# Loading the first x as eight transfers of 16 partitions with step 8

## The chip, the core and the metric

One core of a Trainium2 chip. The metric is the device time of the program in microseconds (us); less is better. A profile also gives the span from the first to the last instruction, about 2 us less than that time (262 against 260.2 us in the profiled run before).

## The reference

```python
batch, m, k, n = 16, 512, 768, 1024
x: [16, 768, 512] float32      y: [16, 768, 1024] float32
np.einsum('bkm,bkn->bmn', x, y).astype(np.float32)
```

Sixteen products of 512 x 768 by 768 x 1024. The core reads 75.5 MB and writes 33.55 MB.

## The kernel before

Row k = 6p + ko of a batch lies in partition p, so each partition of an x is one contiguous run of 12288 bytes in memory, and of a y one of 24576 bytes. All transfers are issued by SyncE (SP), between device memory and the SBUF, the core's buffer of 128 partitions. VectorE (DVE) casts x and y to bf16, TensorE (PE) multiplies, ScalarE (ACT) copies the products out of PSUM, where TensorE leaves them.

```python
    x_v = x.rearrange("b (p ko) m -> b p ko m", ko=KT)      # KT = 6, P = 128
    ...
    def wide_dma(key, dst, src, dram_rows, load):
        if key not in made:                                 # the first of its kind: plain,
            made[key] = nc.sync.dma_start(dst, src)         # one read per partition
            return made[key]
        ...                                                 # later ones: a copy whose reads
                                                            # span dram_rows partitions
    for b in range(B):
        i = b % 2
        if b >= 2:
            nc.sync.wait_ge(cast, nx[b - 2])
        wide_dma("x", xs[i][:], x_v[b], 4, True).then_inc(sx[i], 16)
        if b >= 2:
            nc.sync.wait_ge(cast, nx[b - 2] + parts(b - 2))
        wide_dma("y", ys[i][:], y_v[b], 2, True).then_inc(sy[i], 16)
        if b >= LAG:
            store(b - LAG)
    ...
    for b in range(B):                                      # VectorE
        i = b % 2
        n = 16 * (b // 2 + 1)
        ...
        nc.vector.wait_ge(sx[i], n)
        nc.vector.tensor_copy(xb[:, i], xs[i][:]).then_inc(cast, 1)
        nc.vector.wait_ge(sy[i], n)
        ...
```

The whole kernel:

## Time and profile before

| | before |
|---|---|
| time, median of 3 runs | 262.55 us (262.53 to 262.94) |
| span of the profiled run | 260.2 us |
| share of 16 DMA engines' time filled | 98.3% |
| moved over the span | 419 GB/s |
| first x cast, first y cast begin at | 7.23 us, 14.91 us |

The prediction below shows the lines of this profile. They are to be read in this order: the shares of the engines (none of the compute engines is full), the DMA row (full in all slices but the first and the last), then the start of the stream. In the tables by window a line holds the stretch, its length, five pairs of busy time and number of instructions (PE, PEld, DVE, ACT, POOL), the granted TensorE clock, the DMA share and the GB/s. A packet is counted where it starts, so short windows scatter around the mean.

### The profile page before, as it was taken

The numbers are of one execution on the slowest core, as the hardware profiler recorded it, in microseconds if no ns is written. First come the engines' busy times: TensorE is split into PE (matmuls) and PEld (weight loads), VectorE is DVE, ScalarE is ACT, GpSimd is POOL, SyncE is SP. The second block draws the span as 40 slices with busy tenths as digits, with TensorE's granted clock in tenths as the row PEclk, the third lists the DMA queues.
The fourth block names the chain that finished last, engine by engine and source line by source line (L and its number), as shares of the span: only waits on it lengthen the run. The fifth ranks groups of instructions, "written<-read, shape, count | busy, mean of one in ns | idle before, by whom it ended". The sixth has DMA issues, their size and how long they took to land. (4 is left out here: it accounts for less than half of the span.)

```text
span 260.2 us, 2506 instructions
## 1 busy us (share of the span) xinstructions
PE 188.3 (72%) x768; PEld 90.3 (35%) x768; DVE 82.0 (32%) x33; ACT 61.1 (23%) x33; POOL 0.2 (0%) x4
## 2 busy tenths in 40 slices
PE   0019999998938959499491995949869697785930
PEld 0004555554513525244250352514424243442410
DVE  0261644525241152511425214252232523125000
ACT  1000442243220222203222022220412204031220
POOL 0000000000000000000000000000000000000000
PEclk9999999999995979979999597997968989997985
DMA  7999989999999999999999999999999999999995
GB/s 272 418 476 408 476 378 469 393 368 461 438 398 469 388 479 423 411 441 393 458 431 441 433 388 464 408 436 446 396 456 418 464 416 423 451 385 431 438 403 227
DMA packets 4514, 109.07 MB, mean 419 GB/s; under 512 B 768, under 2 KB 768, under 8 KB 768
## 3 DMA queue, kind: packets, MB, share of 16 engines
q1 hardware_dynamic: 4512, 109.05, 98.3%
q14 instruction: 2, 0.02, 0.0%
HBM read 75.50 MB, written 33.55 MB: 419 GB/s over the span
## 5 line engine op out<-in xcount | busy, mean ns | idle before, releaser
L149 PE MATMUL ps<-yb,xb 128*128 x768 | 188.3, 411 | 61.0 <-PEq L144 61.0
L149 PEld LDWEIGHTS ps<-yb,xb 128*128 x768 | 90.3, 118 | 158.5 <-issue 92.6
L165 ACT COPY ob<-ps 128x2048 f32<-128x2048 f32 x32 | 59.8, 1869 | 184.8 <-PE ps L149 184.8
L127 DVE CAST yb<-ys 128x6144 bf16<-128x6144 f32 (+1 forms) x17 | 53.8, 3171 | 86.5 <-DMA ys<-in_y_dram 86.5
L123 DVE CAST xb<-xs 128x3072 bf16<-128x3072 f32 x16 | 28.2, 1760 | 69.7 <-DMA xs<-in_x_dram 65.2
L165 ACT ACT_TABLE_LOAD x1 | 1.3, 1283 | 5.3 <-issue 5.3
L189 POOL MEMSET const-bfloat16-1.0<- 128x1 bf16 x1 | 0.1, 102 | 0.0
L189 POOL MEMSET const-uint8-127<- 128x1 uint8 x1 | 0.1, 102 | 0.0
L189 POOL MEMSET const-float32-1.0<- 128x1 f32 x1 | 0.1, 99 | 0.0
L189 POOL MEMSET const-float32-0.0<- 128x1 f32 x1 | 0.1, 98 | 0.2 <-issue 0.2
## 6 DMA issues: line engine op xcount, KB each, us to landing
ys<-in_y_dram SPq DMA_DIRECT2D x16, 3072.0 KB, 28.2
out_dram<-ob SPq DMA_DIRECT2D x16, 2048.0 KB, 32.6
xs<-in_x_dram SPq DMA_DIRECT2D x16, 1536.0 KB, 29.8
```

What stands on the lines that cost most here:

```text
L123: nc.vector.tensor_copy(xb[:, i], xs[i][:]).then_inc(cast, 1)
L127: nc.vector.tensor_copy(yb[:, i, ks], ys[i][:, ks]).then_inc(cast, 1)
L149: mm = nc.tensor.matmul(ps[g][:, m, nt], x_w[:, bass.ds(s, 1), kt, mo], yb[:, bass.ds(s, 1), kt, nt * NF:(nt + 1) * NF], start=(kt == 0), ...
L165: cp = nc.scalar.copy(ob[b % NO][:, g * HB:(g + 1) * HB].rearrange("p m (t f) -> p m t f", f=NF), ps[g][:])
L189: nc = _bacc.Bacc("TRN2", target_bir_lowering=False, num_devices=1)
```

## The change

Its intent: with a single transfer of 128 rows some of the DMA engines start up to 1 us later than others (by the packet records ten start at 1.98 to 2.08 us and six at 2.74 to 3.02). Eight transfers of 16 rows were meant to give each of the sixteen engines one row at a time, so that all begin at once. Each transfer adds 16 to the semaphore that VectorE waits for, so the seven further transfers add 112 to the number awaited. A side effect: the x of batch 1 is now the first of its kind, and so loaded plainly.

```diff
+    x_first = x_v[0].rearrange("(a c) k m -> a c k m", c=8)
+    for c in range(8):
+        nc.sync.dma_start(xs[0][c::8], x_first[:, c]).then_inc(sx[0], 16)
     for b in range(B):
         i = b % 2
         if b >= 2:
             nc.sync.wait_ge(cast, nx[b - 2])
-        wide_dma("x", xs[i][:], x_v[b], 4, True).then_inc(sx[i], 16)
+        if b > 0:
+            wide_dma("x", xs[i][:], x_v[b], 4, True).then_inc(sx[i], 16)
 ...
-        nc.vector.wait_ge(sx[i], n)
+        nc.vector.wait_ge(sx[i], n + (112 if i == 0 else 0))
```

## The prediction

Passages that no trace of this case bears out are cut, and the cuts are marked. Packets of a 16-row transfer with step 8 would take twice as long as the 0.46 us of the present load: that factor of two was my assumption, and the profile before did not show it; "sharing" is its name. That small transfers would let the late engines start on time was assumed too. The sum came to +2.7 us for the first x and +0.1 us for the small terms, +2.8 us and so 265.3 us, if packets are twice as long (case a), and to -0.4 us if they are not (case b).

> **What bounds the kernel now.** I read the page first (parts 2, 3, 5), then the chain of waits, then the queue's issues in order of time, then windows of one microsecond at the start and of ten at the end, and last the records of single DMA packets in the trace.
>
> Parts 1 to 3 of the page:
> ```profile
> PE 188.3 (72%) x768; PEld 90.3 (35%) x768; DVE 82.0 (32%) x33; ACT 61.1 (23%) x33; POOL 0.2 (0%) x4
> ...
> DMA  7999989999999999999999999999999999999995
> ...
> q1 hardware_dynamic: 4512, 109.05, 98.3%
> ...
> HBM read 75.50 MB, written 33.55 MB: 419 GB/s over the span
> ```
> No compute engine is full, but the row DMA has a 9 or an 8 in all slices except the first and the last, and the one queue that carries loads and stores fills 98.3% of the time of 16 DMA engines. Each engine moves 109.05 MB / 16 = 6.816 MB. The packet records give the unit costs: 12288 bytes take 460 ns (first x), 24576 bytes 912 ns (first y), 49152 bytes 1837 ns on average (all later loads), 16384 bytes 611 ns (stores). Per engine: 8 x 0.460 + 8 x 0.912 + 90 x 1.837 + 128 x 0.612 = 3.7 + 7.3 + 165.3 + 78.3 = 254.6 us. The first packets start at 1.98 us, so about 257 us is the earliest end. The DMA stream is the bound, and only the start, the end and the rate of the engines are left to win or lose.
>
> The view of the waits says the same from the other side, and the chain that ended last is only the tail:
> ```profile
> DVE yb L127 <- DMA ys<-in_y_dram: 86.5, 16, 5.9
> DVE xb L123 <- DMA xs<-in_x_dram: 65.2, 13, 7.2
> ```
> VectorE waits 152 us for loads. Nothing on the compute side is ever early enough to hold the DMA queue up: the page's part 6 shows loads issued 28 to 30 us before they land, so two to three transfers always stand in the queue.
>
> The start, from the timeline (start, duration, what):
> ```profile
> 0.95 0.39 SPq L72 DMA_DIRECT2D xs<-in_x_dram  x1
> 1.39 0.42 SPq L72 DMA_DIRECT2D ys<-in_y_dram  x1
> 1.86 0.54 SPq L72 DMA_DIRECT2D xs<-in_x_dram  x1
> 2.44 0.62 SPq L72 DMA_DIRECT2D ys<-in_y_dram  x1
> ...
> 7.23 1.76 DVE L123 CAST xb<-xs 128x3072 bf16<-128x3072 f32 x1 [7.23 <-DMA xs<-in_x_dram]
> ...
> 14.91 3.36 DVE L127 CAST yb<-ys 128x6144 bf16<-128x6144 f32 x1 [5.92 <-DMA ys<-in_y_dram]
> ```
> and the windows (last two columns: DMA share, GB/s):
> ```profile
> 1.00:2.00 1.00, 0.00 (x0) 0.00 (x0) 0.00 (x0) 0.00 (x0) 0.00 (x0) 1.00 0.19 37
> 2.00:3.00 1.00, 0.00 (x0) 0.00 (x0) 0.00 (x0) 0.00 (x0) 0.00 (x0) 1.00 0.81 160
> 3.00:4.00 1.00, 0.00 (x0) 0.00 (x0) 0.00 (x0) 0.00 (x0) 0.00 (x0) 1.00 0.83 344
> 4.00:5.00 1.00, 0.00 (x0) 0.00 (x0) 0.00 (x0) 0.00 (x0) 0.00 (x0) 1.00 1.12 479
> ```
> The reader should see that the stream reaches its full rate (some 430 GB/s) only after 3 us. The packet records say why: ten engines start between 1.98 and 2.08 us, but their first packets take 636 to 1516 ns instead of 460; six engines start only between 2.74 and 3.02 us. Eight engines end the first x at 6.09 to 6.46 us, eight at 6.75 to 6.85 us. A clean start would be 1.98 + 8 x 0.46 = 5.66 us. So 0.4 to 1.2 us per engine are lost there, and that is what the change is after.
>
> The end: by the packet records twelve engines end at 256.98 to 257.35 us and four at 257.92 to 258.56 us. The last store is issued at 251.2 us, and several of the faster engines stand idle for 0.3 to 1.1 us around then, because PE and the last copy release it; the slow four never idle, and they set the end.
>
> [...]
> [...] 12288 bytes in 460 ns are 26.7 GB/s per engine, all sixteen at once[...]
> [...] 0.39 us for the issue, first packet 1.03 us after its start, landing at about 7.2 us.
>
> **The change part by part.**
> 1. Removed: one issue of 128 rows (0.39 us). Added: eight of 16 rows, partitions c, c+8, ..., c+120. The cheapest issues of plain transfers here are 0.33 to 0.39 us, with 0.05 us between them, so a step of about 0.44 us. The first y is issued at 0.95 + 8 x 0.44 = 4.5 us instead of 1.39, and its first packets can start at 4.5 + 1.0 = 5.5 us. The engines come to it after 5.7 us at the earliest, so the issues are hidden; at 0.6 us each (like the fourth issue now) y could start only at 6.8 us, about where the late engines start it today.
> 2. [...] the six late engines should start at about 2.0 us: up to 0.8 us won for them[...].
> 3. [...] Then each packet takes about 2 x 0.46 = 0.92 us and the first x takes 8 x 0.92 = 7.4 us instead of 8 x 0.46 = 3.7. From 2.0 us, with some 0.3 us of the cold start left, all engines end it at about 9.7 us, against 6.3 and 6.8: 2.9 to 3.4 us later, call it 2.7 allowing for part of the sharing to go uneven.
> 4. Small terms: seven more semaphore packets per engine, 7 x about 6 ns = 0.04 us. The later loads are copies of the first plain one of their kind with widened reads; now x of batch 1 is that plain one, 8 x 0.460 = 3.68 us instead of 2 x 1.82 = 3.63: 0.05 us. Together 0.1 us.
>
> All this happens in the first 10 us on a stream that never idles later, so a shift of the engines passes to the end one for one; the last y, the last casts, PE and the last store follow the loads by the same amount. The sum is +2.7 + 0.1 = +2.8 us [...] and 0.1 - 0.5 = -0.4 us if not.
>
> **Rivals.**
> (a) [...] 262.55 + 2.8 = 265.3 us. [...]
> (b) No sharing, a clean start: the late engines gain 0.4 to 1.1 us, the early ones 0 to 0.7; the slowest gains about 0.5, less 0.1: 262.1 us. For: late starts are visible. [...]
> (c) The queue starves on the issues: steps of 0.6 us put y at 6.8 us or later, so 0 to 1 us lost: 263 us. For: the third and fourth issues took 0.54 and 0.62 us. Against: these had 128 rows behind 128 rows[...].
> (d) The gain is hidden by the end: if the chain over PE and the last store set the end, nothing would come through. It follows the last load, which shifts as well, so I give it little.
>
> **Range and chances.** I give (a) 60%, (b) and (d) 28%, (c) 12%. The prediction is the middle of the likelier case, 265.1 us; the range must reach from the clean start, 261.8, to full sharing with the whole cold start kept, 266.2. The 2% limits are 257.3 and 267.8 us; no case comes near either: within 2% 0.96, slower 0.03, faster 0.01.
>
> **What would show it right or wrong.** Right: eight issues of about 0.4 us from 0.95 us; sixteen engines starting near 2.0 us; packets of the first x at about 0.9 us and only some 215 GB/s between 3 and 9 us; the first x cast beginning at about 10 us and the first y cast at about 17.6 us instead of 14.91; all DMA after that as before. Wrong: packets of 460 ns in the first x and its cast before 7.2 us (then (b)), or gaps between the packets (then (c)). A change of the rate in the middle of the stream, where nothing was touched, would be outside of this reasoning.

## The result, and the profile after

| | before | after |
|---|---|---|
| time, median of 4 runs each | 262.54 us (262.36 to 262.94) | 266.34 us (265.98 to 266.74) |
| ratio | | 1.0143 (1.0123 to 1.0162) |
| span of the profiled run | 260.2 us | 264.6 us |
| first x cast, first y cast begin at | 7.23, 14.91 us | 11.02, 18.85 us |

A ratio is the mean time of one kernel's fast runs over that of the other's of the same rounds, so it isn't quite the ratio of the medians quoted. The loss is 3.8 us. The prediction said 265.1 us and a range up to 266.2; the time lies 0.14 us above the range, and the loss is half as large again as the 2.55 us forecast.

The page after, DMA parts:

```profile
DMA  6999998999999899899999999899998999999993
...
q1 hardware_dynamic: 4720, 109.06, 97.7%
...
HBM read 75.50 MB, written 33.55 MB: 412 GB/s over the span
```

The stream is as full as before nearly everywhere. "Busy" tells nothing of the loss: a slow packet counts as busy for as long as it takes. The bytes do tell.

The start, from the timeline after:

```profile
0.95 5.04 SPq L104 DMA_DIRECT2D xs<-in_x_dram  x8
...
6.03 0.58 SPq L72 DMA_DIRECT2D ys<-in_y_dram  x1
...
11.02 1.76 DVE L128 CAST xb<-xs 128x3072 bf16<-128x3072 f32 x1 [11.02 <-DMA xs<-in_x_dram]
...
18.85 3.36 DVE L132 CAST yb<-ys 128x6144 bf16<-128x6144 f32 x1 [6.07 <-DMA ys<-in_y_dram]
```

Eight issues take 5.04 us, 0.63 us from one to the next, where the prediction had 0.44. The first x is there 3.8 us later than before, the first y 3.9 us later: the whole loss is there before the first matmul.

The stretch from 4 to 9 us, before and then after:

```profile
4.00:9.00 5.00, 0.00 (x0) 0.00 (x0) 1.76 (x1) 1.28 (x1) 0.00 (x0) 1.00 1.04 447
```
```profile
4.00:9.00 5.00, 0.00 (x0) 0.00 (x0) 0.00 (x0) 1.28 (x1) 0.00 (x0) 1.00 1.04 218
```

The DMA share is 1.04 in both, the rate 447 against 218 GB/s. The packet records show the same one by one: of the 128 packets of the first x, the last 96 to start took 831 to 989 ns (before: 460 for nearly all). The 32 before them were shorter (458 to 871 ns).

The end, from the chain that ended last, before and then after:

```profile
237.05 12.25 PE ps L149 x48
...
249.33 1.87 ACT ob L165
```
```profile
241.37 10.74 PE ps L154 x48
...
252.13 1.87 ACT ob L170
```

The last matmuls begin 4.3 us later and the last copy 2.8 us later, because TensorE was granted a higher clock in the last batch after (1.00 against 0.86, 10.74 us for the same 48 matmuls instead of 12.25). That did not help: by the packet records the slowest DMA engine lands its last store at 263.33 us after and 258.93 us before, some 3 and 1.5 us behind the median engine, and the program waits for it (SyncE's last wait for stores: 4.1 us after, 2.5 before).

### The profile page after: what moved, and what is told of

Its sections match the earlier page's. It is cut to its first block, busy times and chain, and to the rows that moved or that the text cites. A ratio compares the mean times of both kernels' runs of the same rounds, so it can differ in the third digit from the quotient of the medians.

```text
span 264.6 us, 2513 instructions
## 1 busy us (share of the span) xinstructions
PE 187.7 (71%) x768; PEld 90.1 (34%) x768; DVE 82.0 (31%) x33; ACT 61.1 (23%) x33; POOL 0.2 (0%) x4
```

## The experiments

The theory: which partitions a transfer names sets the time of its packets. How much was my assumption before the runs: with 16 rows of step 8 twice the 0.46 us of the kernel before, with 16 contiguous rows four times, with step 7 mostly once. No trace shows a mechanism that would give these factors; the figures that stand without a rival's name are those of the theory. Rivals: the eight issues and small transfers themselves; the distance of the rows in memory; something of the start of the program only; and the side effect on the x of batch 1. Ten kernels were run, all of them as variants of the two above. Times are medians, "before" is that of the same call.

| run | first x is loaded as | time | before | ratio (95%) |
|---|---|---|---|---|
| a1_after_again | 8 x 16 rows, step 8 (the change) | 266.06 | 262.31 | 1.0144 (1.0127 to 1.0161) |
| a2_step1 | 8 x 16 rows, contiguous | 270.02 | 262.31 | 1.0283 (1.0266 to 1.0300) |
| a3_step7 | 7 x 16 rows, step 7, and 16 contiguous | 264.68 | 262.31 | 1.0087 (1.0070 to 1.0104) |
| a4_hbm_rows | as the change; memory rows contiguous (wrong result) | 265.94 | 262.31 | 1.0137 (1.0120 to 1.0153) |
| b1_late | as before; batch 8 as in the change | 266.70 | 262.67 | 1.0156 (1.0138 to 1.0174) |
| b2_step4 | 4 x 32 rows, step 4 | 263.10 | 262.67 | 1.0017 (0.9997 to 1.0037) |
| b3_free6 | 6 x 128 rows of 2048 bytes | 262.92 | 262.67 | 1.0017 (0.9994 to 1.0040) |
| b4_before_again | as before | 262.77 | 262.67 | 1.0000 (0.9982 to 1.0018) |
| c1_halves | 2 x 128 rows of 6144 bytes | 262.60 | 262.56 | 1.0005 (0.9992 to 1.0019) |
| c2_x1_plain | as before; x of batch 1 plain | 262.54 | 262.56 | 1.0001 (0.9987 to 1.0014) |

### The change again, for a second profile

No edit.

> The changed kernel itself, unaltered, for a second profile beside its variants. If the loss is fixed by the program: 266.0 to 266.7 us again, first-x packets near 0.9 us, the median engine 3.0 us later than before from batch 5 on. Open: whether one engine again lags the median by 3 us at the end. If that lag is chance of one execution, it differs in this profile while the median does not; if it belongs to the changed start, it is there again.

The time is 266.06 us. In the packet records the median engine lands the first y at 17.73 us (first profile after: 17.74; before: 14.39). The slowest engine again ends about 3 us behind the median (2.9; in the first profile 3.1). The loss is the program's, not one execution's.

Both profiles of the change also show that the packets that start fifth (65th to 80th by start) are shorter: their median is 0.86 and 0.85 us in the two profiles, against 0.95 and 0.94 us for the sixteen before them and 0.94 to 0.95 us for the last 32. Why was not shown.

### Contiguous rows

```diff
-    x_first = x_v[0].rearrange("(a c) k m -> a c k m", c=8)
     for c in range(8):
-        nc.sync.dma_start(xs[0][c::8], x_first[:, c]).then_inc(sx[0], 16)
+        rows = slice(16 * c, 16 * c + 16)
+        nc.sync.dma_start(xs[0][rows], x_v[0, rows]).then_inc(sx[0], 16)
```

> The same eight transfers of 16 rows, but partitions 16c to 16c+15 instead of every eighth. [...] first-x packets of about 1.84 us instead of 0.93, the first x ends at about 17 us instead of 9.8, the time is 266.3 + 7.4 = 273.7 us. Rival, cost of eight issues and small transfers: the issues are the same, so 266.3 us and packets of 0.93 us.

The same number of transfers of the same size, other partitions. In the timeline and the window from 4 to 12 us:

```profile
0.94 3.64 SPq L104 DMA_DIRECT2D xs<-in_x_dram  x8
...
15.66 1.76 DVE L128 CAST xb<-xs 128x3072 bf16<-128x3072 f32 x1 [15.66 <-DMA xs<-in_x_dram]
```
```profile
4.00:12.00 8.00, 0.00 (x0) 0.00 (x0) 0.00 (x0) 1.28 (x1) 0.00 (x0) 1.00 1.02 121
```

The issues are even cheaper than with step 8 (0.46 us from one to the next instead of 0.63), and the kernel is 4.0 us slower. From the third packet of each engine on, a packet took 1.60 to 1.64 us, and the rate fell to 121 GB/s. So the number of issues isn't the cause; which partitions a transfer names is. The size was a miss: I had expected 1.84 us and 273.7 us. The 1.84 us was four times 0.46, an assumption; why the packets took less was not shown.

### Step 7

```diff
-    x_first = x_v[0].rearrange("(a c) k m -> a c k m", c=8)
-    for c in range(8):
-        nc.sync.dma_start(xs[0][c::8], x_first[:, c]).then_inc(sx[0], 16)
+    for c in range(7):
+        nc.sync.dma_start(xs[0][c:112:7], x_v[0, c:112:7]).then_inc(sx[0], 16)
+    nc.sync.dma_start(xs[0][112:], x_v[0, 112:]).then_inc(sx[0], 16)
```

> Seven transfers of 16 rows with step 7 and a last one of the 16 contiguous rows left over. [...] most packets take 0.46 us and a few 0.92; the last transfer has [...] 1.84 us. The issues of 0.63 us then set the pace, the first x ends at about 8.5 us instead of 9.8, and the time is about 265.0 us. Rival, cost of eight issues: 266.3 us. Rival, the step in memory or in the buffer at all: packets of 0.93 us as with step 8.

Seven of the eight transfers now name every seventh partition, the last one 16 contiguous ones. From the timeline:

```profile
0.94 4.43 SPq L103 DMA_DIRECT2D xs<-in_x_dram  x7
5.42 0.58 SPq L104 DMA_DIRECT2D xs<-in_x_dram  x1
...
10.39 1.76 DVE L128 CAST xb<-xs 128x3072 bf16<-128x3072 f32 x1 [10.39 <-DMA xs<-in_x_dram]
```

The time is 264.68 us (expected: about 265.0), with as many issues and the same 0.63 us between them as in the change. The packets of the first seven transfers mostly took 0.46 to 0.84 us, a few up to 1.2: shorter than with step 8, but not the clean 0.46 for most of them that I had expected. The first x ended later than expected (its cast at 10.39 us); why was not shown. In no run did all packets of 16-row transfers take 0.46 us, so a part of what stands above 0.46 us here (the median of the first seven transfers is 0.63 us, as long as the step of the issues) may belong to 16-row transfers as such. It is too small to explain the 0.94 us of step 8.

### Contiguous rows in memory, step 8 in the SBUF

Its output is wrong, which doesn't matter for the time.

```diff
-    x_first = x_v[0].rearrange("(a c) k m -> a c k m", c=8)
     for c in range(8):
-        nc.sync.dma_start(xs[0][c::8], x_first[:, c]).then_inc(sx[0], 16)
+        nc.sync.dma_start(xs[0][c::8], x_v[0, 16 * c:16 * c + 16]).then_inc(sx[0], 16)
```

> Wrong result on purpose: partitions c, c+8, ... as in the changed kernel, but the rows read from memory are 16 contiguous ones. [...] nothing changes, packets 0.93 us, 266.3 us. Rival, the memory side (rows 98 KB apart read by 16 engines at once): packets fall towards 0.46 us and the time to about 264 us, where the pace of the issues holds it.

```profile
4.00:9.00 5.00, 0.00 (x0) 0.00 (x0) 0.00 (x0) 1.28 (x1) 0.00 (x0) 1.00 1.00 216
```

216 GB/s between 4 and 9 us and 265.94 us: nothing changed (the change: 218 GB/s, 266.06 us). The distance of the rows in memory is ruled out; what matters is which partitions are written: with the same rows read, contiguous partitions (a2_step1) gave 270.02 us. The issues stay at 0.59 us each too, against 0.42 us there, so the step of the partitions, not that of the rows in memory, made these issues dearer.

### The same in the middle of the stream

```diff
-        wide_dma("x", xs[i][:], x_v[b], 4, True).then_inc(sx[i], 16)
+        if b == 8:
+            x_eight = x_v[b].rearrange("(a c) k m -> a c k m", c=8)
+            for c in range(8):
+                nc.sync.dma_start(xs[i][c::8], x_eight[:, c]).then_inc(sx[i], 16)
+        else:
+            wide_dma("x", xs[i][:], x_v[b], 4, True).then_inc(sx[i], 16)
 ...
-        nc.vector.wait_ge(sx[i], n)
+        nc.vector.wait_ge(sx[i], n + (112 if i == 0 and b >= 8 else 0))
```

> The first x is loaded as before; the x of batch 8 is loaded as eight transfers of 16 rows with step 8, while two to three transfers stand ahead of it in the queue. [...] each engine's part takes 8 x 0.94 = 7.5 us instead of 2 x 1.82 = 3.6, nothing else idles, so 262.4 + 3.9 = 266.3 us. Rival, the loss belongs to the start (pace of the issues, [...] late first packets): the issues are hidden behind the queue here, so 262.4 us.

The window from 111 to 117 us, in which these packets run, and the same window of the kernel before (second profile):

```profile
111.00:117.00 6.00, 6.00 (x30) 3.17 (x28) 0.00 (x0) 0.83 (x1) 0.00 (x0) 1.00 1.15 260
```
```profile
111.00:117.00 6.00, 4.68 (x14) 1.99 (x15) 0.80 (x1) 0.00 (x0) 0.00 (x0) 0.72 1.01 434
```

260 GB/s instead of 434, and a loss of 4.0 us (3.9 expected). The issues, from the timeline:

```profile
85.51 6.30 SPq L109 DMA_DIRECT2D xs<-in_x_dram  x8
```

They ran from 85.5 us on and the data only from 110 us on, so neither the pace of the issues nor the start of the program has any part in it. This is the cleanest measurement of what the partitions of step 8 cost: 4.0 us at the end for one x of 1536 KB.

### Four transfers of 32 rows with step 4

```diff
-    x_first = x_v[0].rearrange("(a c) k m -> a c k m", c=8)
-    for c in range(8):
-        nc.sync.dma_start(xs[0][c::8], x_first[:, c]).then_inc(sx[0], 16)
+    x_first = x_v[0].rearrange("(a c) k m -> a c k m", c=4)
+    for c in range(4):
+        nc.sync.dma_start(xs[0][c::4], x_first[:, c]).then_inc(sx[0], 16)
```

The wait in VectorE has 48 instead of 112. Two cases were expected, packets as in the change or packets as in the 128-row transfer.

> Four transfers of 32 rows with step 4[...]. [...] as in the changed kernel: packets 0.93 us, 266 us. [...] in the 128-row transfer: packets 0.46 us, the first x ends near 5.5 us, 262 us.

```profile
4.00:9.00 5.00, 0.00 (x0) 0.00 (x0) 0.71 (x1) 1.28 (x1) 0.00 (x0) 1.00 1.05 401
```

401 GB/s between 4 and 9 us, and 263.10 us, not to be told from the kernel before. 45 of the 48 packets that started second to fourth took 458 to 495 ns; later some took up to 1.2 us, for which I have no cause. So most packets of 32 rows with step 4 are as short as those of 128 rows; how the rows are given out to the engines the records do not show. The expected gain down to 262 us did not come: the issues, 0.63 us apart, bring 32 rows, 24.6 KB for each of 16 engines on the mean, which take them 2 x 0.46 = 0.92 us (no limit), but the first packets are still long (0.5 to 1.1 us).

### Six transfers over all partitions, and two

```diff
-    x_first = x_v[0].rearrange("(a c) k m -> a c k m", c=8)
-    for c in range(8):
-        nc.sync.dma_start(xs[0][c::8], x_first[:, c]).then_inc(sx[0], 16)
+    for k in range(KT):
+        nc.sync.dma_start(xs[0][:, k], x_v[0, :, k]).then_inc(sx[0], 16)
```

The wait has 80 instead of 112.

> Six transfers, each of all 128 partitions with one sixth of the row (2048 bytes). [...] six issues of about 0.42 us do not starve the queue; the first x ends at 6 to 7 us and the time is 262.0 to 262.8 us. Rival, several transfers instead of one cost the 4 us: 265 to 266 us.

262.92 us: six transfers that each name all partitions cost nothing to speak of (ratio 1.0017). Its window from 4 to 9 us:

```profile
4.00:9.00 5.00, 0.00 (x0) 0.00 (x0) 0.81 (x1) 1.28 (x1) 0.00 (x0) 1.00 1.04 370
```

The first x ended at 6.8 to 7.9 us, a little later than I had expected; 2048 bytes took 84 ns, 24.4 GB/s per engine instead of 26.7.

The same with two halves of 6144 bytes, an attempt to get what the change wanted:

```diff
-    x_first = x_v[0].rearrange("(a c) k m -> a c k m", c=8)
-    for c in range(8):
-        nc.sync.dma_start(xs[0][c::8], x_first[:, c]).then_inc(sx[0], 16)
+    for h in range(2):
+        ks = slice(h * KH, (h + 1) * KH)
+        nc.sync.dma_start(xs[0][:, ks], x_v[0, :, ks]).then_inc(sx[0], 16)
```

The wait has 16 instead of 112.

> An attempt to keep what the change wanted [...]: the first x as two transfers of all 128 partitions, half a row (6144 bytes) each. [...] the issues are short (0.4 us). [...] the first x ends up to 0.5 us earlier and the time is about 262.1 us; if the first microsecond is slow whatever is asked for, it is 262.5 us like the kernel before. [...]

262.60 us against 262.56: no gain. Some of the sixteen earliest packets took 0.9 to 1.1 us although 6144 bytes need 0.23 later on, and the first y packets start between 6.29 and 7.05 us (before: 6.09 to 6.85). The first microsecond is slow with these pieces too, so they did not help. What makes it slow was not shown.

### The kernel before again, and the side effect on batch 1

> The kernel before, unaltered, for a second profile: 262.4 us. Open: whether the 0.45 us that all engines lost together at 55 to 57 us in its first profile is there again (then the program causes it) or not (then it was chance of that execution, and the shift between the two streams is 3.3 us for the median engine all along).

262.77 us. In this profile too the engines lose time together at 56 to 58 us:

```profile
56.00:58.00 2.00, 2.00 (x11) 1.02 (x9) 0.00 (x0) 0.19 (x1) 0.00 (x0) 1.00 0.61 238
```

The median engine needed 11.25 us between the landings of the fourth y and of the fifth, 11.44 in the first profile before, and 10.99 and 11.00 in the two profiles after. Two more profiles begin as the kernel before does and differ here: 11.59 us in c2_x1_plain, 11.08 in b1_late. So the kernels with the old start gave away 0.1 to 0.6 us here that the two with the new start did not, which returns a little of the loss to the median engine. I have no cause for it. The lag of the slowest engine at the last y, on the other hand, was 1.8 us in the first profile before, 2.9 in this one, 3.1 and 2.8 in the two after: the large difference of the first two profiles there was chance.

```diff
-        wide_dma("x", xs[i][:], x_v[b], 4, True).then_inc(sx[i], 16)
+        if b == 1:
+            nc.sync.dma_start(xs[i][:], x_v[b]).then_inc(sx[i], 16)
+        else:
+            wide_dma("x", xs[i][:], x_v[b], 4, True).then_inc(sx[i], 16)
```

> The kernel before, with only the side effect of the change: the x of batch 1 is read in rows of 12288 bytes instead of 49152. By packet times 8 x 0.460 instead of 2 x 1.815 us per engine, 0.05 us more: 262.5 us, not to be told from the kernel before. If this part carried the loss, 1 us or more would show.

262.54 us against 262.56. The side effect carries nothing that can be measured.

## Why the prediction was right and wrong

Right: the DMA stream is the bound, and a shift at its start goes through to the end, though not quite one for one (the median engine is 3.35 us later at the first y and 2.7 to 3.0 us at the last); the rate depends on the partitions named: packets took 0.46 us with all 128, about 0.9 with 16 of step 8 and 1.6 with 16 contiguous ones (why was not shown, and the factor of two was assumed); the packets of the first x take about 0.9 us and the rate falls to about 215 GB/s (218 measured); the side effects are negligible. The experiment at batch 8 shows the slower packets alone, at 4.0 us.

Wrong was the size of the shift, at two steps. Part 3 worked out 2.9 to 3.4 us for the first x and then wrote "call it 2.7 allowing for part of the sharing to go uneven"; and the sum let the y and all after it follow "by the same amount". The first x came 3.0 us later, the end of the first y 3.4 us later on the mean engine and 3.9 us later on the slowest. The records of the first profiles, as means over the engines, give these terms:

| term | before | after | difference | in the prediction |
|---|---|---|---|---|
| first packet starts | 2.34 us | 2.59 us | +0.25 | 0 or a gain |
| from there to the end of the first x | 4.23 us | 7.01 us | +2.78 | with the start, 2.9 to 3.4, shaved to 2.7 |
| first packet of y | 0.91 us | 1.31 us | +0.40 | left out |
| end of the first y | 13.93 us | 17.35 us | +3.42 | 2.8 |

So the shaving missed 0.33 us (3.03 against 2.7), and the first packet of y, which the sum left out, 0.40 us. Without it the sum would have been 3.0 to 3.5 us, still short of 3.8. The first 32 packets were indeed less slow (458 to 871 ns); none of the last 96 came near 460 (831 to 989).

That the unshaved term fits the first x is partly luck. It had the engines start near 2.0 us and take 7.7 us (7.4, and 0.3 of the cold start); they started at 2.59 us on average and took 7.01.

The first row: the issue of a step-8 transfer took up to 0.62 us, not 0.33 to 0.39, and the first packets came later (2.37 us instead of 1.98). The hoped-for gain of the late engines was used up by that. The third row: the first y packets are longer after than before; the records show no cause. They are there in other runs too: with contiguous rows the first y packets took 1.87 us on average, and after the slow x of batch 8 the next loads of 49152 bytes began with packets of 2.1 to 2.5 us instead of 1.82. The first 32 packets of x are shorter than the 96 after them, 0.65 against 0.92 us on the mean; whether the two belong together was not shown.

The slowest engine lost half a microsecond more, 3.9 us at the landing of the first y. By following packets that join end to end I find that in both kernels a fetch of instructions of 8192 bytes came between its packets (at 10.84 us before, at 11.89 after), with a long packet after it (1451 ns before, 1574 after, where 912 is usual). Before, it was one of the eight engines that had ended the first x early (6.3 us, with 6.6 the mean), which made up for part of that; after, it ended the first x at 9.7 us, no earlier than the mean. That assignment is inferred, as the records don't name engines. At the end, over three profiles of kernels like before (last landing 258.93, 260.01, 259.39 us) and two after (263.33, 262.74), the shift is 3.6 us; the timed runs say 3.8.

The rivals: (c) named the pace of the issues, and it did turn out 0.63 us, but from the 33rd on the packets took 0.83 to 0.99 us, longer than that, so only the first packets show it. (b) had 28% together with (d); the variants that cost nothing (step 4, six pieces, halves) gained nothing either, so no gain was there for (d) to hide.

## What to carry to other kernels

When a stream fills all DMA engines, look at GB/s and at the time of single packets, not at the busy share: it was 1.04 at 447 GB/s and at 218. Transfers of 16 partitions, every eighth or contiguous ones, brought the rate of the whole core at the start down from 447 GB/s to 218 and 121, and where it was tried in the middle of the program (every eighth) from 434 to 260; splits along the row in six and in two, and one into 32 partitions with step 4, cost nothing that could be measured (ratios 1.0017, 1.0005 and 1.0017). In an estimate, don't shave a worked-out term by a feeling, and follow a delay into the first packets of the next transfer: the two were worth 0.33 and 0.40 us here.
